# A float32 decoder trunk on one core: four of eight K pairs in seven products, a second block sum by an accumulating transfer, a longer lag at the turns, and grouped half-array products

## The chip, the cores and the metric

The kernel runs on one core of a Trainium2 chip. The metric is the device time of one execution in microseconds, taken as the median of several runs. A profile is one further execution, recorded by the hardware profiler; its rows give the line of the kernel, the engine and the operation. TensorE (PE) multiplies, VectorE (DVE) and ScalarE (ACT) do the work on elements, GpSimd (POOL) does a little of it and issues the accumulating transfers, SyncE (SP) issues the other transfers.

## The reference, cut to what matters

Two decoder layers over 256 tokens of width 2048, in float32. Layer 0 mixes by a chunked state-space scan, layer 1 by differential attention; each is followed by a SwiGLU feed-forward part, with an RMS norm before and after every part.

```python
for i in range(DEPTH):                       # DEPTH = 2
    h = rmsnorm(x, norm_mix_pre[i])
    m = ssd_mixer(h, ...) if i % 2 == 0 else diff_attention(h, ...)
    x = x + rmsnorm(m, norm_mix_post[i])
    h = rmsnorm(x, norm_ffn_pre[i])
    x = x + rmsnorm(swiglu(h, ffn_w_gate[i], ffn_w_up[i], ffn_w_down[i]), norm_ffn_post[i])

def swiglu(h, w_gate, w_up, w_down):         # 2048 -> 5632 -> 2048
    return (jax.nn.silu(h @ w_gate) * (h @ w_up)) @ w_down
```

In the scan, `y_diag` is for each head (width 64) a 128 x 128 matrix of decays times the head's values, for each of two chunks of 128 tokens. In the attention, each of 16 heads has two score matrices of head width 64; their softmaxes are subtracted with a weight.

## The kernel before

**Precision.** Every float32 weight block is cut into two parts in a format that TensorE multiplies in one pass: `hi`, a copy by ACT (L133), and `lo`, the rest, by a subtraction on DVE (L134). Function `prep` does this for one raw tile of up to four blocks of 128 x 512. A product of activations and weights is three matmuls: hi x hi, hi x lo, lo x hi. After the scan, `hi` and `lo` have four buffers each, all preparations use them in turn, and the first operation of a preparation waits until TensorE has done the last product with the tile that held the buffer. Raw tiles come from `raw_tile`: three buffers of `rawp`, and in the feed-forward stage two of `mpool` as well (then the tile is named `rawm`).

**Plain products.** `mv` computes 256 tokens (two token tiles t = 0, 1) against one chunk of 512 columns. The products of t = 0 run as each half tile of weights is ready; those of t = 1 are put in a queue `pending` and run `lag` steps later. So at the end of a chunk the result of t = 0 is complete first. `out_proj` uses `mv` for its last columns (n = 3 for the last one, L719) with the lag it is given, LAG2 = 2; the feed-forward part's first chunk uses LAG = 4. When the last chunk of a token tile is complete, `norm_chain` normalizes it, adds it to the residual stream `x`, transposes it through TensorE (`ptx`) and writes the next activations `xT`; `stats` (L640) sums the squares of the new `x` for the next norm two steps later.

**Products of pairs.** For gate and up (columns 0 to 9 of 11 chunks) and for a part of the down projection, `pair` computes two token tiles x two column chunks at once, a K pair (two blocks of 128 of the contraction) at a time, eight K pairs for gate and up. A plain K pair needs 8 block products, so 24 matmuls. For the K pairs in SEVEN it uses the scheme that multiplies 2 x 2 blocks in seven products, so 21 matmuls: four sums of weight blocks are formed at run time, and four sums of activation blocks, the "forms" (`make_form`, once per layer; `keep` stores them in DRAM, and they are loaded again through POOL's queue at the beginning of parts 1 and 2, L878). The forms live in four buffers with the tag `xr`, which the forms of the down projection use too. The steps of one K pair in seven products are, in `pair`:

- SP loads the four blocks into `raw` (L244); POOL then issues a transfer that adds a block onto `raw[:, 0]` (L247);
- first preparation: `hi` and `lo` of `raw[:, 1:4]` (the blocks as they are, 1536 wide), L259;
- three sums on DVE in place (L261 to L263);
- second preparation: `hi` and `lo` of all of `raw` (the sums, 2048 wide), L264;
- nine matmuls with the first preparation, then twelve with the second. Four of the products go into sums of their own in PSUM (tiles `cp`), the others straight into the results.

After the last K pair in seven products DVE combines the `cp` tiles (L276 to L280), and after K pair 7 `done` adds them to the results; for gate ACT then applies SiLU, for up DVE multiplies. After each up pair the products are transposed into the activations of the down projection (`act_piece`).

**Order.** Weight chunks go in three parts (PARTS): gate and up of some chunks, then the down projection of those, accumulated in DRAM. The order of instructions on each engine is fixed when the program is built; an engine does its own instructions strictly in that order and waits on semaphores. `later(k, fn)` puts work k steps (`tick`) ahead.

**Scan and attention.** `scan_group` runs, interleaved with the products of the next chunks, `diag(0)` at step 6 and `diag(1)` at step 7: 16 small products each whose output is 64 partitions (L543). In `attention_group`, `softmax(t, hp)` computes the scores of two heads of one token tile by products over 64 partitions (L963), masks them, and takes the softmax; it is called for four combinations of t and hp.

```python
            if kp in seven:
                nc.gpsimd.dma_start(raw[:, 0:1], src[0][:, 1:2], accum_op=ALU.add)
```

Of the kernel before, what the change touches and what calls it, by code (L numbers as in the profile page):

```python
# [10 lines left out]
F32 = mybir.dt.float32  # L11
F32R = mybir.dt.float32r
AF = mybir.ActivationFunctionType
ALU = mybir.AluOpType
# [15 lines left out]
LAG = 4  # L30
LAG2 = 2

SEVEN = (2, 4, 6)


PARTS = [((10, 0, 1), (20, 0, 21, 1, 2, 3), {0: (21,), 2: (21, 2)}),
# [5 lines left out]
def trunk_kernel(ctx, tc, x_rows, x_cols, vec_cols, vec64, post_rows, lam_rows,  # L42
# [19 lines left out]
    def aux(name):  # L62
        return auxp.tile([P, 512], F32, tag="aux", name=name)
# [156 lines left out]
    def pair(blocks, stat, seven, form, done):  # L220

        flush()
        acc = {}
        end = len(blocks) - 1  # L230

        def mm(k, st, hi, lo, last):
            first = k not in acc
            if first:
                acc[k] = (auxp.tile([P, 512], F32, tag="aux", name="cp") if isinstance(k, str) else
                          accp.tile([P, 512], F32, tag="acc", name="acc"))
            for q, (a, b) in enumerate(((st[0], hi), (st[0], lo), (st[1], hi))):
                nc.tensor.matmul(acc[k], a, b, start=first and q == 0, stop=last and q == 2)  # L238

        ss = {}  # L240
        for kp, src in enumerate(blocks):
            raw = raw_tile()
            for c in range(2):
                nc.sync.dma_start(raw[:, 2 * c:2 * c + 2], src[c])  # L244
            if kp in seven:

                nc.gpsimd.dma_start(raw[:, 0:1], src[0][:, 1:2], accum_op=ALU.add)  # L247
# [12 lines left out]

            nc.vector.tensor_tensor(raw[:, 2], raw[:, 2], raw[:, 0], op=ALU.add)  # L261
            nc.vector.tensor_tensor(raw[:, 3], raw[:, 3], raw[:, 2], op=ALU.add)  # L262
            nc.vector.tensor_tensor(raw[:, 1], raw[:, 2], raw[:, 1], op=ALU.subtract)  # L263
            sh, sl = prep(raw)  # L264
            mm("p1", stat(kp, 0, 0), hi[:, 1], lo[:, 1], last)
            mm((0, 0), stat(kp, 1, 0), hi[:, 2], lo[:, 2], False)
            mm((0, 1), form(kp, 3), hi[:, 0], lo[:, 0], False)
            tick()
            mm("p6", form(kp, 2), sh[:, 2], sl[:, 2], last)
            mm("p5", form(kp, 0), sh[:, 1], sl[:, 1], last)  # L270
            mm("p7", form(kp, 1), sh[:, 0], sl[:, 0], last)
            mm((1, 0), stat(kp, 1, 1), sh[:, 3], sl[:, 3], False)
            tick()
            if last:
                s1, u, w, x = (t512(n) for n in ("s1", "su", "sw", "sx"))
                nc.scalar.copy(s1, acc["p1"])  # L276
                nc.vector.tensor_tensor(u, acc["p6"], s1, op=ALU.subtract)
                nc.vector.tensor_tensor(w, acc["p5"], u, op=ALU.add)
# [241 lines left out]
    def scan_group(g, st, mts):  # L520
# [59 lines left out]
            nc.vector.tensor_tensor(yo, pyo.rearrange("p (h d) -> p h d", h=8), exb(1), op=ALU.mult)  # L580

        later(5, lambda: (tokens(0), tokens(1)))
        later(6, lambda: (diag(0), to_state()))
        later(7, lambda: (diag(1), turn(0)))
        later(9, new_state)
        later(10, off)
        later(11, lambda: turn(1))
# [27 lines left out]
    def norm_chain(t, ss4, last_mw, step, final, t512):  # L615

        rn = rstd_of(ss4[:, 3:4], D, f"post{step}_{t}", ss4[:, 0:1])
        for n in range(4):
            mw = last_mw if n == 3 else m[(t, n)]
            xt = xres[(t, n)]  # L620
            if final and n == 0:
                nc.scalar.activation(mw, mw, AF.Copy, scale=rn)
                nc.gpsimd.tensor_tensor(xt, xt, mw, op=ALU.add)
            else:
                nc.vector.scalar_tensor_tensor(xt, mw, rn, xt, op0=ALU.mult, op1=ALU.add)  # L625
            if final:
                nc.sync.dma_start(out[t * P:(t + 1) * P, n * 512:(n + 1) * 512], xt)
                continue
            pt = aux("ptx")
            for j in range(4):  # L630
                nc.tensor.transpose(pt[:, j * P:(j + 1) * P], xt[:, j * P:(j + 1) * P], ident)  # L631
            for j in range(4):
                sl = slice(t * P, (t + 1) * P)
                sc = pre_cols[step + 1][:, 4 * n + j:4 * n + j + 1]
                pj = pt[:, j * P:(j + 1) * P]
                nc.scalar.activation(xT_hi[n][:, j, sl], pj, AF.Copy, scale=sc)  # L636
                nc.vector.scalar_tensor_tensor(xT_lo[n][:, j, sl], pj, sc, xT_hi[n][:, j, sl].bitcast(F32),
                                               op0=ALU.mult, op1=ALU.subtract)
# [12 lines left out]
    def out_proj(w, first, last, acts, kgs, step, final, lag, t512, pw, scale=None, ns=range(4), two={}, forms=None, md=None, mid=None):  # L651

# [46 lines left out]
        for n in ns:  # L699
            def evac(t, ps, n=n):  # L700
# [220 lines left out]
    def attention_group(hg):  # L921
# [30 lines left out]

        prT, es, sms = {}, {}, {}

        def softmax(t, hp):
            nk, ts = t + 1, slice(t * P, (t + 1) * P)
            qT, kT = qk[(0, hp)], qk[(1, hp)]

            sc = [aux(f"sc{c}")[:, :2 * nk * P].rearrange("p (h k) -> p h k", h=2) for c in range(2)]
            for h in range(2):  # L960
                for c in range(2):
                    cp = slice(c * 64, (c + 1) * 64)
                    nc.tensor.matmul(sc[c][:, h], qT[cp, h, ts], kT[cp, h, :nk * P], start=True, stop=True)  # L963
            mx = small.tile([P, 2, 2], F32, tag="mx", name="mx", bufs=4)
            sm = small.tile([P, 2, 2], F32, tag="sm", name="sm", bufs=4)
            e = []
            for c in range(2):
                nc.vector.tensor_tensor(sc[c][:, :, ts], sc[c][:, :, ts],
                                        causal.unsqueeze(1).to_broadcast([P, 2, P]), op=ALU.add)
                nc.vector.tensor_reduce(mx[:, c], sc[c], axis=AX.X, op=ALU.max)  # L970
                nc.vector.tensor_scalar(mx[:, c], mx[:, c], qsc[t], -1.0, op0=ALU.mult, op1=ALU.mult)
                e.append(t512("e", (P, 2, nk * P)))
                for h in range(2):
# [3 lines left out]
            for h in range(2):  # L977
# [4 lines left out]
            es[(t, hp)] = e[0]  # L982

        def turn(t, hp):
            nk, e = t + 1, es[(t, hp)]
# [101 lines left out]
```

## Time and profile before

| | us |
|---|---|
| median of 3 runs (2560.80 to 2561.73) | 2561.22 |
| the profiled execution's own time | 2560.26 |
| its span, first to last instruction | 2558.5 |

The span is the time between the first and the last instruction of the record; the 1.8 us around it are start and end. A row of the lists by line has the engine, the operation, the tile written and the tiles read, the shape, the count, then busy time and mean length, then the idle time of the engine before these instructions and who ended it. A row in order of time has start, length, engine, line and operation; what stands in brackets is the idle time before it and what ended it. Two more rows of the page belong to the stages that the change touches, the software queue (the transfers that POOL issues) and the hardware queue:

```profile
q1 hardware_dynamic: 125296, 502.91, 56.8%
q0 software_dynamic: 16416, 33.04, 6.9%
```

The columns are packets, MB, and the time of the packets as a share of the span on 16 DMA engines.

### The profile page before, as it was taken

To read this page: it belongs to the slowest core of one execution; us is meant where nothing else is said; L and a number is where in the kernel's file an instruction comes from. 1 tells how busy PE (TensorE), PEld (TensorE's weight loads), DVE (VectorE), ACT (ScalarE), POOL (GpSimd) and SP (SyncE) were. 2 spreads that over 40 slices of the span, in tenths; PEclk is the share of its full clock that TensorE was granted. 3 is DMA by queue.
4 is the path that set the end of the run, shared out by engine and by line. 5 is a ranking of instruction groups with operands and counts; after the bars stand their busy time and mean duration, and the time that the engine had idled before them with its cause. 6 is when DMAs were issued, how large, how long until landed. Compare 5 with 4: busy or idle time off the path is not lost. (4 is left out here: it accounts for less than half of the span.)

```text
span 2558.5 us, 31249 instructions
## 1 busy us (share of the span) xinstructions
PE 2527.4 (99%) x11860; PEld 2069.1 (81%) x11860; DVE 1908.9 (75%) x2297; ACT 1363.9 (53%) x1656; POOL 237.1 (9%) x222
## 2 busy tenths in 40 slices
PE   9999999999999999999999999999999999999998
PEld 7877888787878888888887778887788888888886
DVE  6777547776687888977886765656578879878985
ACT  5767556665565454554544654444555455545553
POOL 0121000120110000011002100000100000010003
PEclk9999999999999999999999999999999999999999
DMA  7545555454776776777677544444676866796675
GB/s 275 198 165 181 189 191 195 167 180 165 273 259 209 250 242 202 242 235 238 198 244 231 205 147 166 167 157 142 235 227 212 276 217 214 229 261 216 208 248 166
DMA packets 142518, 538.78 MB, mean 211 GB/s; under 512 B 14304, under 2 KB 31008, under 8 KB 114976
## 3 DMA queue, kind: packets, MB, share of 16 engines
q1 hardware_dynamic: 125296, 502.91, 56.8%
q0 software_dynamic: 16416, 33.04, 6.9%
q8 instruction: 93, 1.52, 0.3%
q10 hardware_dynamic: 656, 0.85, 0.1%
q14 instruction: 57, 0.47, 0.1%
HBM read 516.74 MB, written 17.89 MB: 209 GB/s over the span
## 5 line engine op out<-in xcount | busy, mean ns | idle before, releaser
L134 DVE TENSOR_TENSOR lo<-raw,hi 128x2048 fp32r<-128x2048 f32 (+2 forms) x451 | 855.7, 1906 | 381.9 <-ACT hi L133 377.1
L133 ACT CAST hi<-raw 128x2048 fp32r<-128x2048 f32 (+2 forms) x451 | 698.8, 1557 | 600.4 <-DVE raw L263 190.3
L187 PE MATMUL acc<-hi,xT 128*128 128x512 f32 x1792 | 590.3, 400 | 4.7 <-ACT xT L636 2.1
L238 PE MATMUL acc<-hi,xT 128*128 128x512 f32 x1840 | 589.3, 390 | 0.0
L238 PEld LDWEIGHTS acc<-hi,xT 128*128 128x128 f32 x1840 | 345.3, 188 | 71.5
L187 PEld LDWEIGHTS acc<-hi,xT 128*128 128x128 f32 x1792 | 335.8, 188 | 81.1 <-issue 5.9
L238 PE MATMUL acc<-lo,xT 128*128 128x512 f32 x920 | 358.0, 389 | 0.0
L187 PE MATMUL acc<-lo,xT 128*128 128x512 f32 x896 | 352.0, 393 | 1.8 <-DVE lo L134 1.8
L134 DVE TENSOR_TENSOR lo<-rawm,hi 128x2048 fp32r<-128x2048 f32 (+1 forms) x115 | 248.2, 2158 | 71.3 <-ACT hi L133 67.7
L133 ACT CAST hi<-rawm 128x2048 fp32r<-128x2048 f32 (+1 forms) x115 | 207.7, 1806 | 171.3 <-DVE rawm L263 108.4
L238 PEld LDWEIGHTS acc<-lo,xT 128*128 128x128 f32 x920 | 172.7, 188 | 35.6
L187 PEld LDWEIGHTS acc<-lo,xT 128*128 128x128 f32 x896 | 168.8, 188 | 38.4 <-issue 3.6
L238 PE MATMUL acc<-hi,ah_f 128*128 128x512 f32 x468 | 183.1, 391 | 0.0
L238 PE MATMUL acc<-hi,al_f 128*128 128x512 f32 x468 | 182.2, 389 | 0.0
L238 PE MATMUL acc<-lo,ah_f 128*128 128x512 f32 x468 | 182.1, 389 | 0.0
L212 PE MATMUL acc<-xT,hi 128*128 128x512 f32 x512 | 180.1, 397 | 0.0
L238 PE MATMUL cp<-hi,ff 128*128 128x512 f32 x468 | 156.9, 389 | 0.0
L214 PE MATMUL acc<-xT,lo 128*128 128x256 f32 x512 | 142.7, 280 | 0.0
L138 DVE SCALAR_TENSOR_TENSOR lo<-raw,cols,hi 128x512 fp32r<-128x512 f32 x128 | 91.6, 763 | 55.8 <-ACT hi L137 55.7
L212 PEld LDWEIGHTS acc<-xT,hi 128*128 128x128 f32 x512 | 96.1, 188 | 22.9
L137 ACT ACTIVATE hi<-raw,cols 128x512 fp32r<-128x512 f32 x128 | 84.6, 715 | 53.6 <-PE acc L187 36.7
L238 PEld LDWEIGHTS acc<-hi,al_f 128*128 128x128 f32 x468 | 87.8, 188 | 18.2
(279 smaller groups left out, 3491.0 us busy)
## 6 DMA issues: line engine op xcount, KB each, us to landing
raw<-in_w_zxbc_dram SPq DMA_DIRECT2D x80, 1024.0 KB, 4.8
raw<-in_w_d_dram SPq DMA_DIRECT2D x98, 512.0 KB, 5.7
raw<-in_w_g_dram SPq DMA_DIRECT2D x96, 512.0 KB, 5.8
raw<-in_w_u_dram SPq DMA_DIRECT2D x96, 512.0 KB, 5.8
raw<-in_w_qkv_dram SPq DMA_DIRECT2D x48, 1024.0 KB, 4.8
raw<-in_w_so_dram SPq DMA_DIRECT2D x32, 1024.0 KB, 4.8
rawm<-in_w_g_dram SPq DMA_DIRECT2D x64, 512.0 KB, 5.8
rawm<-in_w_u_dram SPq DMA_DIRECT2D x64, 512.0 KB, 6.2
```

The lines of the kernel that those rows point to most:

```text
L133: nc.scalar.copy(hi, raw)
L134: nc.vector.tensor_tensor(lo, raw, hi.bitcast(F32), op=ALU.subtract)
L137: nc.scalar.activation(hi[:, j], raw[:, j], AF.Copy, scale=scale[j])
L138: nc.vector.scalar_tensor_tensor(lo[:, j], raw[:, j], scale[j], hi[:, j].bitcast(F32), op0=ALU.mult, op1=ALU.subtract)
L187: nc.tensor.matmul(acc[t], a, b[:, j], start=(i == 0 and j == 0 and q == 0), stop=(i == last and j == 1 and q == 2))
L212: nc.tensor.matmul(acc[ct], hi[:, j, cs], x.rearrange("p a s -> p (a s)"), start=(i == 0 and j == 0), stop=False)
L214: nc.tensor.matmul(acc[ct][:, :S], lo[:, j, cs], x[:, 0], start=False, stop=(i == last and j == 1))
L238: nc.tensor.matmul(acc[k], a, b, start=first and q == 0, stop=last and q == 2)
```

## The change

SEVEN becomes (1, 3, 4, 6), so each gate pair and each up pair computes four K pairs in seven products and one more form is made and kept per layer. In every K pair in seven products, those of the down projection too, a second accumulating transfer adds `src[0][:, 0]` onto `raw[:, 2]` after the first preparation has read it, and two sums on DVE remain; the places of two of the sums in the tile are exchanged, and so are their uses.

```diff
-SEVEN = (2, 4, 6)
+SEVEN = (1, 3, 4, 6)
...
             hi, lo = prep(raw[:, 1:4])
 
-            nc.vector.tensor_tensor(raw[:, 2], raw[:, 2], raw[:, 0], op=ALU.add)
-            nc.vector.tensor_tensor(raw[:, 3], raw[:, 3], raw[:, 2], op=ALU.add)
-            nc.vector.tensor_tensor(raw[:, 1], raw[:, 2], raw[:, 1], op=ALU.subtract)
+            nc.gpsimd.dma_start(raw[:, 2:3], src[0][:, 0:1], accum_op=ALU.add)
+            nc.vector.tensor_tensor(raw[:, 1], raw[:, 1], raw[:, 2], op=ALU.add)
+            nc.vector.tensor_tensor(raw[:, 3], raw[:, 3], raw[:, 1], op=ALU.add)
             sh, sl = prep(raw)
...
-            mm("p6", form(kp, 2), sh[:, 2], sl[:, 2], last)
-            mm("p5", form(kp, 0), sh[:, 1], sl[:, 1], last)
+            mm("p6", form(kp, 2), sh[:, 1], sl[:, 1], last)
+            mm("p5", form(kp, 0), sh[:, 2], sl[:, 2], last)
```

In the scan, `diag(1)` moves one step earlier, to stand with `diag(0)`. At the turns, the statistics come five steps later instead of two, and the last chunk of the last output projection has the lag 4.

```diff
-        later(6, lambda: (diag(0), to_state()))
-        later(7, lambda: (diag(1), turn(0)))
+        later(6, lambda: (diag(0), diag(1), to_state()))
+        later(7, lambda: turn(0))
...
-            later(2, stats)
+            later(5, stats)
...
-            mv([w[n, kg // 2] for kg in up[::2]], up_stat, evac, lag,
+            mv([w[n, kg // 2] for kg in up[::2]], up_stat, evac, LAG if last and n == 3 else lag,
```

In the attention, `softmax` takes a list of head pairs; for token tile 0 the two calls become one over four heads, with tiles twice as wide, for token tile 1 they stay two.

```diff
-        def softmax(t, hp):
-            nk, ts = t + 1, slice(t * P, (t + 1) * P)
-            qT, kT = qk[(0, hp)], qk[(1, hp)]
+        def softmax(t, hps):
+            nk, ts, nh = t + 1, slice(t * P, (t + 1) * P), 2 * len(hps)
...
-            for h in range(2):
+            for h in range(nh):
+                qT, kT = qk[(0, hps[h // 2])], qk[(1, hps[h // 2])]
...
-        softmax(0, 0)
-        later(1, lambda: softmax(0, 1))
-        later(2, lambda: (turn(0, 0), softmax(1, 0)))
-        later(3, lambda: (turn(0, 1), softmax(1, 1)))
+        softmax(0, (0, 1))
+        later(2, lambda: (turn(0, 0), softmax(1, (0,))))
+        later(3, lambda: (turn(0, 1), softmax(1, (1,))))
```

More of the change, by code (lines that the diff above doesn't have):

```diff
@@ L953, in attention_group @@
         prT, es, sms = {}, {}, {}
-        def softmax(t, hp):
-            nk, ts = t + 1, slice(t * P, (t + 1) * P)
-            qT, kT = qk[(0, hp)], qk[(1, hp)]
-            sc = [aux(f"sc{c}")[:, :2 * nk * P].rearrange("p (h k) -> p h k", h=2) for c in range(2)]
-            for h in range(2):
+        def softmax(t, hps):
+            nk, ts, nh = t + 1, slice(t * P, (t + 1) * P), 2 * len(hps)
+            sc = [aux(f"sc{c}")[:, :nh * nk * P].rearrange("p (h k) -> p h k", h=nh) for c in range(2)]
+            for h in range(nh):
+                qT, kT = qk[(0, hps[h // 2])], qk[(1, hps[h // 2])]
                 for c in range(2):
                     cp = slice(c * 64, (c + 1) * 64)
-                    nc.tensor.matmul(sc[c][:, h], qT[cp, h, ts], kT[cp, h, :nk * P], start=True, stop=True)
-            mx = small.tile([P, 2, 2], F32, tag="mx", name="mx", bufs=4)
-            sm = small.tile([P, 2, 2], F32, tag="sm", name="sm", bufs=4)
+                    nc.tensor.matmul(sc[c][:, h], qT[cp, h % 2, ts], kT[cp, h % 2, :nk * P], start=True, stop=True)
+            mx = small.tile([P, 2, 4], F32, tag="mx", name="mx", bufs=4)[:, :, :nh]
+            sm = small.tile([P, 2, 4], F32, tag="sm", name="sm", bufs=4)[:, :, :nh]
             e = []
@@ L968, in softmax @@
                 nc.vector.tensor_tensor(sc[c][:, :, ts], sc[c][:, :, ts],
-                                        causal.unsqueeze(1).to_broadcast([P, 2, P]), op=ALU.add)
+                                        causal.unsqueeze(1).to_broadcast([P, nh, P]), op=ALU.add)
                 nc.vector.tensor_reduce(mx[:, c], sc[c], axis=AX.X, op=ALU.max)
                 nc.vector.tensor_scalar(mx[:, c], mx[:, c], qsc[t], -1.0, op0=ALU.mult, op1=ALU.mult)
-                e.append(t512("e", (P, 2, nk * P)))
-                for h in range(2):
+                e.append(t512("e", (P, nh, nk * P)))
+                for h in range(nh):
                     nc.scalar.activation(e[c][:, h], sc[c][:, h], AF.Exp, scale=qsc[t], bias=mx[:, c, h:h + 1],
@@ L976, in softmax @@
             nc.vector.reciprocal(sm, sm)
-            for h in range(2):
+            for h in range(nh):
                 nc.vector.tensor_scalar(e[1][:, h], e[1][:, h], sm[:, 1, h:h + 1], neglam,
@@ L981, in softmax @@
                                                op0=ALU.mult, op1=ALU.add)
-            es[(t, hp)] = e[0]
+            for i, hp in enumerate(hps):
+                es[(t, hp)] = e[0][:, 2 * i:2 * i + 2]
         def turn(t, hp):
```

## The prediction

> **What bounds the kernel now.** I read the page first (busy shares, granted clock), then the busy time by stage, then the waits of TensorE, then one pair of weight chunks in order of time on ACT, DVE and PE.
>
> ```profile
> span 2558.5 us, 31249 instructions
> PE 2527.4 (99%) x11860; PEld 2069.1 (81%) x11860; DVE 1908.9 (75%) x2297; ACT 1363.9 (53%) x1656; POOL 237.1 (9%) x222
> PEclk9999999999999999999999999999999999999999
> ```
>
> ```profile
> core 0: us, PE busy (x) PEld busy (x) DVE busy (x) ACT busy (x) POOL busy (x), PEclk, DMA share, GB/s
> 757.20:1372.50 615.30, 614.99 (x2753) 508.97 (x2752) 513.73 (x485) 308.13 (x217) 44.21 (x54) 1.00 0.72 228
> 897.50:939.00 41.50, 41.50 (x185) 34.35 (x183) 33.75 (x28) 19.84 (x13) 2.62 (x3) 1.00 0.79 246
> 980.50:1024.00 43.50, 43.50 (x201) 35.91 (x199) 38.35 (x45) 20.43 (x18) 2.60 (x3) 1.00 0.63 203
> ```
>
> TensorE is busy all the time at full clock. The first window is the whole FFN pair stage of layer 0 (615 us; layer 1 has an equal one). One gate pair or up pair takes 41.5 us (second window); where activations are also turned for the down projection it takes 43.5 and DVE is busy for 38.35 of them (third window). So the end is set by the number of products, as long as ACT and DVE hand over `hi` and `lo` in time. How close that is, one gate pair shows; its columns are start, length, engine and line:
>
> ```profile
> 916.56 0.39 PE L238 MATMUL cp<-hi,xT 128*128 128x512 f32 x1
> ...
> 928.80 0.39 PE L238 MATMUL cp<-hi,ff 128*128 128x512 f32 x1
> 929.02 0.39 PE L238 MATMUL cp<-lo,ff 128*128 128x512 f32 x1
> ```
>
> ```profile
> 916.80 1.48 ACT L133 CAST hi<-rawm 128x1536 fp32r<-128x1536 f32 x1 [2.25 <-issue]
> 922.29 1.92 ACT L133 CAST hi<-rawm 128x2048 fp32r<-128x2048 f32 x1 [4.01 <-DVE rawm L263]
> 924.11 1.90 ACT L133 CAST hi<-raw 128x2048 fp32r<-128x2048 f32 x1
> ```
>
> ```profile
> 918.32 1.76 DVE L134 TENSOR_TENSOR lo<-rawm,hi 128x1536 fp32r<-128x1536 f32 x1 [1.04 <-ACT hi L133]
> 920.11 0.69 DVE L261 TENSOR_TENSOR rawm<-rawm 128x512 f32<-128x512 f32 x1
> 920.84 0.69 DVE L262 TENSOR_TENSOR rawm<-rawm 128x512 f32<-128x512 f32 x1
> 921.45 0.68 DVE L263 TENSOR_TENSOR rawm<-rawm 128x512 f32<-128x512 f32 x1
> 924.24 2.29 DVE L134 TENSOR_TENSOR lo<-rawm,hi 128x2048 fp32r<-128x2048 f32 x1 [2.11 <-ACT hi L133]
> ```
>
> This is K pair 4, in seven products. Successive products start 0.227 us apart (928.80, 929.02), though each is drawn 0.39 long. The first preparation (`hi`, 1536 wide) starts at 916.80, just after PE began the products of another K pair at 916.56 and so was done with a buffer: `hi` and `lo` have four buffers, and a preparation starts when PE releases the fourth before it. From there the chain is `hi` 1.48, `lo` 1.76, three sums 2.0, `hi` of all four 1.92, `lo` 2.29: it ends at 926.53, 9.7 us after its start. PE wants this `lo` at 929.02. **The slack is 2.5 us.** Behind it PE waited almost never:
>
> ```profile
> PE ptx L631 <- DVE x L625: 3.2, 5, 1.5
> PE acc L187 <- ACT xT L636: 2.1, 3, 1.5
> ...
> PE acc L187 <- DVE xT L637: 1.5, 2, 1.1
> ...
> PE cp L238 <- DVE lo L134: 0.3, 1, 0.3
> ```
>
> ```profile
> 1022.27 2.29 DVE L134 TENSOR_TENSOR lo<-rawm,hi 128x2048 fp32r<-128x2048 f32 x1 [2.39 <-ACT hi L133]
> ...
> 1024.62 0.50 PE L238 MATMUL cp<-lo,ff 128*128 128x512 f32 x1 [0.29 <-DVE lo L134]
> ```
>
> The last row is the same place in the window of 43.5 us: there the slack is already nil.
>
> **The change, part by part.** *Products.* A seven-product K pair needs 21 products where a plain one needs 24. SEVEN grows from three to four, in 5 column pairs x gate and up x 2 layers = 20 calls: 60 products less, x 0.227 = **-13.6 us**.
>
> *Work of DVE and ACT.* By the starts in the rows above a seven-product K pair costs DVE 1.79 + 2.0 + 2.21 = 6.0 us now and 1.79 + 1.4 + 2.21 = 5.4 with two sums, a plain one 2.21. A call goes from 5 x 2.21 + 3 x 6.0 = 29.1 to 4 x 2.21 + 4 x 5.4 = 30.4: the transfer does not make DVE lighter than before, it only pays for most of the fourth. ACT gets one more `hi` of 1.48 per call. Both fit in TensorE's time (33.75 + 1.3 of 40.8; 38.35 + 1.3 of 42.8) if nobody waits. The extra form per layer (four small DVE operations and a split, some 3 us) and its reload lie beside products as well; that all four `xr` buffers now hold forms makes the down projection's form wait until the up pair has passed K pair 1, tens of us ahead of its use. I cost these at nothing; uncovered, they would be 2 x 3 us.
>
> *The new wait.* The second accumulating transfer overwrites a block that both halves of the first preparation read, so it is issued after that `lo`, and the two remaining sums wait for its landing. It lies in the chain. Before, the one accumulating transfer came ahead of the first preparation and hid there. Its length stands in the issues by line (count, KB, median us from issue to landing), and the hand-over from DVE to POOL in a wait of another transfer (909.99 + 0.68 to 910.96):
>
> ```profile
> raw<-in_w_g_dram POOLq DMA_DIRECT2D x18, 256.0 KB, 6.2
> raw<-in_w_u_dram POOLq DMA_DIRECT2D x18, 256.0 KB, 4.1
> ...
> raw<-in_w_d_dram POOLq DMA_DIRECT2D x14, 256.0 KB, 7.2
> rawm<-in_w_g_dram POOLq DMA_DIRECT2D x12, 256.0 KB, 5.6
> ...
> rawm<-in_w_u_dram POOLq DMA_DIRECT2D x12, 256.0 KB, 4.2
> ```
>
> ```profile
> 909.99 0.68 DVE L263 TENSOR_TENSOR rawm<-rawm 128x512 f32<-128x512 f32 x1
> ```
>
> ```profile
> 910.96 0.88 POOL L247 DMA_DIRECT2D raw<-in_w_g_dram  x1 [6.60 <-DVE rawm L263]
> ```
>
> The mean over the 60 gate and up transfers is 5.0 us; with 0.3 of hand-over the wait is 5.3, bounded by 4.4 (up) and 6.5 (gate). One sum of 0.6 falls away, so the chain grows by 4.7 to 14.4 us. Against a slack of 2.4 that is an **excess of 2.3 us** for each tight K pair (1.4 to 3.5).
>
> Which are tight: count PE's products from the release of the buffer to the second preparation's first use. With (1, 3, 4, 6) the K pairs 3, 4 and 6 have 21 + 24 + 9 = 54 products, 12.3 us, as K pairs 4 and 6 have today; K pair 1 has 12 + 24 + 24 + 9 = 69, 15.7 us, and just gets through. When PE has waited at 3, K pair 4, whose buffer was free before that, gains as much cover and passes; 6, whose buffer is freed by 3, waits again. Two waits a call: 20 x 2 x 2.3 = **+92 us**. In the crowded calls the slack is nil, but there DVE has other work to put into the wait; I price them like the others (at 4.3 each they would add 32).
>
> The down projection's calls use the same code. Their seven-product K pairs that stand two places after another one have the 54 products too, four a layer; the transfers of `w_d` take 7.2 us: 7.2 + 0.3 - 0.6 - 2.4 = 4.5 us each, x 8 = **+36 us** (0 to 48).
>
> Queues: behind the waiting sums DVE holds the `lo` of later K pairs, PSUM sums and SwiGLU products; behind the waiting transfer POOL holds the first accumulating transfers of later K pairs and the form reloads, needed only for the second `hi`. SP's next loads wait some 5 us longer for a raw buffer, of which there are five. The software queue carries 33.04 MB; 118 transfers of 256 KB more double it, on DMA engines now busy for 0.72 of the stage, so landings get later rather than earlier.
>
> *Lag and statistics at the turns.* The three waits for `x` and `xT` above sum to 6.8 us over the three turns. More products of token tile 1 left over while tile 0 is normalized can cover part: I take **-3** (0 to -7; up to +2 if the longer lag holds `hi` and `lo` back).
>
> *Half-array grouping.* Entering the 64-column products costs 0.32 us (129.38 to 129.70) where the next product otherwise starts after 0.23:
>
> ```profile
> 129.15 0.39 PE L187 MATMUL acc<-lo,xT 128*128 128x512 f32 x1
> 129.38 0.40 PE L187 MATMUL acc<-hi,xT 128*128 128x512 f32 x1
> 129.70 1.09 PE L543 MATMUL py<-mt,xdt 128*64 128x128 f32 x16
> ```
>
> Eight entries fewer in the scan and four in attention: **-1 us** (-3 to +5, if the grouped scores wait for the last K columns in each of four groups). The Trainium skill, TensorEngine Tiling (Array Packing), Key Properties, says that changing the tiling mode drains TensorE; the 0.09 us extra here is what such a drain would come to, so its grouping advice is worth no more than this term.
>
> **Sum**: 92 + 36 - 13.6 - 3 - 1 = +110 us on the profiled execution's own 2560.3 us (its span of 2558.5 and 1.8 around it; the median shown is 1 us more): **2671 us**.
>
> **Rivals.** *The wait is covered* (faster): PE and DVE are given other work meanwhile, such as the nine first products of K pair 4 (2.0 us) ahead of K pair 3's last twelve, or half a plain K pair (2.7 us). That decides when the cover reaches 2.3 us, or the wait falls below 3.0. For it: products into different sums do not depend on each other, and DVE already does another K pair's `lo` between two sums of a call:
>
> ```profile
> 941.36 0.68 DVE L277 TENSOR_TENSOR su<-cp,s 128x512 f32<-128x512 f32 x1
> 941.96 2.28 DVE L134 TENSOR_TENSOR lo<-rawm,hi 128x2048 fp32r<-128x2048 f32 x1
> 944.16 0.69 DVE L278 TENSOR_TENSOR sw<-cp,su 128x512 f32<-128x512 f32 x1
> ```
>
> Against: landings of 4.1 to 7.2 us, and DVE's small reserve. It gives 2560 - 13.6 - 4 = 2543 (2536 to 2555). The Trainium skill, DMA: Bandwidth & Descriptors, Anatomy of one DMA — SWDGE (gpsimd) path, would side with it: 2.0 us plus the bytes at 436 GB/s, an estimate of 2.6 us for 256 KB, below the point above, and thus no excess. This trace disagrees with 4.1 us or more for each of these groups.
>
> *The preparations stay in line* (much slower): if ACT does no later `hi` while it waits for the sums, each seven-product K pair holds it for 1.4 + 1.8 + 5.3 + 1.4 + 1.8 + 0.3 = 12 us.
>
> ```profile
> 1020.33 1.91 ACT L133 CAST hi<-rawm 128x2048 fp32r<-128x2048 f32 x1 [5.51 <-DVE rawm L263]
> ```
>
> That row speaks for it: ACT stood 5.5 us before the second `hi` and took no later one meanwhile; at 922.29 it stood 4.0 us, and the next plain K pair came only at 924.11. A call is then 4 x 1.8 + 4 x 12 = 55 us against 41.5: +13.7 x 20 = +274, with the down projection's 36 and without the 13.6 (TensorE no longer bounds), some 2870 (2790 to 2950). Against it: ACT may have had no better choice there, since the waits were short.
>
> *Hidden just enough* (no change): one wait of 0.7 us a call eats the saving: 2556 to 2566.
>
> **How the numbers follow.** About 0.2% (5 us) is what a measurement of this kernel can tell from no change. Forecast (2600 to 2790, from the bounds of the excess, one to three waits a call) 0.50; covered 0.25; no change 0.06; in line 0.19. So faster 0.25, same 0.06, slower 0.69. The range of 8 in 10 leaves out the line case: 2537 to 2795.
>
> **What would show it.** Right: TensorE waits on `cp` for `lo` (0.3 us now) grow to tens of us, twice a call, and the second sum transfer lands 4 us or more after its issue. Calls of 41 us or less with PE still at 99% would show the cover; calls of 55 us with ACT idle behind the sums would show the line. If landings shrink or the engines' order changes, the excess of 2.3 us is wrong.

## The result, and the profile after

| | us | ratio to before |
|---|---|---|
| before, runs beside these (2560.80 to 2563.17) | 2561.47 | |
| changed (3246.14 to 3250.94) | 3249.04 | 1.2677 [1.2662, 1.2693] |

The kernel is 27% slower, 688 us. The page of the changed kernel (span, busy times, granted clock in 40 slices), its longest waits of TensorE (us in total, times, longest), and the busy times in the window that was the whole feed-forward pair stage of layer 0 before:

```profile
span 3245.8 us, 31519 instructions
PE 2746.9 (85%) x11800; PEld 2178.7 (67%) x11800; DVE 1926.5 (59%) x2269; ACT 1387.7 (43%) x1678; POOL 336.3 (10%) x344
PEclk9999999999898888887889999999898888888888
```

```profile
PE cp L238 <- ACT hi L133: 421.5, 93, 7.4
PE cp L238 <- DVE lo L134: 21.8, 14, 1.8
PE pt_f L291 <- DVE g L824: 13.0, 2, 6.9
```

```profile
core 0: us, PE busy (x) PEld busy (x) DVE busy (x) ACT busy (x) POOL busy (x), PEclk, DMA share, GB/s
757.00:1372.00 615.00, 466.54 (x1750) 361.14 (x1750) 334.57 (x305) 206.19 (x146) 59.82 (x71) 0.86 0.57 165
```

Before, PE was busy for all of that window at full clock; now it is busy for 467 of 615 us at a clock of 0.86, and the stage takes 961 us instead of 615 (first pair product at 759.1, the next plain chunk at 1720.1); in layer 1 it takes 962 instead of 615. So the whole loss lies in the two pair stages, and outside them things got a little better. TensorE waits mostly for `hi` (93 waits, 421.5 us), not for `lo` (14 waits, 21.8 us), and it waits on `cp` 107 times, about once in each of the 98 K pairs in seven products, where the prediction counted two a call and eight in the down projection, 48. The shares of the three engines all fall, PE's from 99 to 85%, DVE's from 75 to 59, ACT's from 53 to 43. When all are less busy at once, look for work that passes from one to the other in a line.

Where the line stands still is seen among the waits of DVE:

```profile
DVE raw L262 <- DMA raw<-in_w_g_dram: 146.1, 24, 8.7
DVE raw L262 <- DMA raw<-in_w_u_dram: 145.1, 24, 9.3
DVE rawm L262 <- DMA rawm<-in_w_g_dram: 108.8, 16, 8.9
DVE rawm L262 <- DMA rawm<-in_w_u_dram: 95.6, 16, 9.5
DVE raw L262 <- DMA raw<-in_w_d_dram: 94.9, 14, 10.9
...
DVE rawm L262 <- DMA rawm<-in_w_d_dram: 34.1, 4, 10.7
```

L262 is the first sum behind the second transfer. It stood still 98 times, once in every seven-product K pair, 624.6 us in all, nine tenths of the loss. One of these in order of time, DVE and then ACT (start, length, engine, line, and the idle time before it):

```profile
1084.72 2.29 DVE L134 TENSOR_TENSOR lo<-raw,hi 128x2048 fp32r<-128x2048 f32 x1 [2.08 <-ACT hi L133]
1086.93 1.75 DVE L134 TENSOR_TENSOR lo<-rawm,hi 128x1536 fp32r<-128x1536 f32 x1
1094.24 0.69 DVE L262 TENSOR_TENSOR rawm<-rawm 128x512 f32<-128x512 f32 x1 [5.56 <-DMA rawm<-in_w_u_dram]
1094.97 0.69 DVE L263 TENSOR_TENSOR rawm<-rawm 128x512 f32<-128x512 f32 x1
1097.75 2.29 DVE L134 TENSOR_TENSOR lo<-rawm,hi 128x2048 fp32r<-128x2048 f32 x1 [2.08 <-ACT hi L133]
```

```profile
1084.60 1.47 ACT L133 CAST hi<-rawm 128x1536 fp32r<-128x1536 f32 x1
1095.82 1.90 ACT L133 CAST hi<-rawm 128x2048 fp32r<-128x2048 f32 x1 [9.76 <-DVE rawm L263]
1097.62 1.89 ACT L133 CAST hi<-raw 128x2048 fp32r<-128x2048 f32 x1
```

DVE ends the first `lo` at 1088.68 and does nothing until the transfer has landed; ACT does nothing from 1086.07 to 1095.82 and takes the next K pair's `hi` (1097.62) only afterwards. Both engines work in program order, and the waiting instruction holds all later preparations. **The length of this line** can be added up by starts. From the first sum to the second `lo` it is 1097.75 - 1094.24 = 3.5 us, then 2.2 to the next `lo`, 1.75 for a first `lo`, and the wait from there to the sum, 6.9 on the mean of the 80 in gate and up: 14.3 us for a seven-product K pair. A plain one puts 2.2 us into the line. The end of a call puts in 8 sums and SwiGLU products (gate) or 12 (up) of 0.6 to 0.7 us, 6.4 on the mean. With the three sums of before, the same sum goes by the rows from 918.32 to 926.45: 8.1 us. Now set this against TensorE's products at 0.227 us, for one call:

| one call of gate or up | line, us | products, us | measured |
|---|---|---|---|
| before: 3 x 8.1 + 5 x 2.2 + 6.4 | 41.7 | 41.5 | 41.9 |
| changed: 4 x 14.3 + 4 x 2.2 + 6.4 | 72.4 | 40.9 | 72.8 |

Measured is the mean of the same four calls of layer 0 (the spacing of their L276 copies). The line gives the new length without TensorE. The row of changed takes its wait of 6.9 us from the same run, so it says where the time lies and does not foretell it; the tests are the runs below. And the line says something of before that the share of busy time did not show: there it was already as long as the products. In these four calls of before DVE was busy for 141.6 us and waited 24.4 for `hi`, 166.0 of 167.5 us:

```profile
897.50:1065.00 167.50, 167.21 (x745) 138.07 (x744) 141.59 (x137) 85.39 (x62) 10.12 (x12) 1.00 0.71 226
```

```profile
DVE lo L134 <- ACT hi L133: 24.4, 15, 2.4
```

### The profile page after: what moved, and what is told of

Read it like the earlier page. It is cut to its first block, busy times and chain, and to the rows that moved or that the text cites. A ratio compares the mean times of both kernels' runs of the same rounds, so it can differ in the third digit from the quotient of the medians.

```text
span 3245.8 us, 31519 instructions
## 1 busy us (share of the span) xinstructions
PE 2746.9 (85%) x11800; PEld 2178.7 (67%) x11800; DVE 1926.5 (59%) x2269; ACT 1387.7 (43%) x1678; POOL 336.3 (10%) x344
## 5 line engine op out<-in xcount | busy, mean ns | idle before, releaser
L133 ACT CAST hi<-raw 128x2048 fp32r<-128x2048 f32 (+2 forms) x463 | 713.2, 1550 | 920.8 <-DVE raw L263 403.6
L134 DVE TENSOR_TENSOR lo<-raw,hi 128x2048 fp32r<-128x2048 f32 (+2 forms) x463 | 870.5, 1889 | 384.0 <-ACT hi L133 378.4
L238 PE MATMUL cp<-hi,ff 128*128 128x512 f32 x588 | 299.5, 573 | 421.5 <-ACT hi L133 421.5
L238 PEld LDWEIGHTS cp<-hi,ff 128*128 128x128 f32 x588 | 155.9, 281 | 491.1 <-ACT hi L133 461.2
L238 PEld LDWEIGHTS acc<-hi,xT 128*128 128x128 f32 x1600 | 328.3, 207 | 112.6 <-ACT hi L133 39.7
L187 PEld LDWEIGHTS acc<-hi,xT 128*128 128x128 f32 x1792 | 335.9, 188 | 74.8 <-issue 4.9
L187 PE MATMUL acc<-lo,xT 128*128 128x512 f32 x896 | 352.7, 394 | 5.4 <-DVE lo L134 5.4
L238 PE MATMUL acc<-lo,xT 128*128 128x512 f32 x800 | 319.5, 399 | 0.0
L262 DVE TENSOR_TENSOR raw<-raw 128x512 f32<-128x512 f32 x62 | 42.9, 692 | 386.0 <-DMA raw<-in_w_g_dram 146.1
L187 PEld LDWEIGHTS acc<-lo,xT 128*128 128x128 f32 x896 | 168.8, 188 | 44.4 <-DVE lo L134 9.7
L238 PE MATMUL cp<-lo,ff 128*128 128x512 f32 x294 | 163.7, 557 | 21.8 <-DVE lo L134 21.8
L238 PEld LDWEIGHTS acc<-lo,xT 128*128 128x128 f32 x800 | 157.3, 197 | 35.3 <-DVE lo L134 0.2
L262 DVE TENSOR_TENSOR rawm<-rawm 128x512 f32<-128x512 f32 x36 | 24.9, 692 | 238.5 <-DMA rawm<-in_w_g_dram 108.8
```

What stands on the lines that cost most here:

```text
L133: nc.scalar.copy(hi, raw)
L134: nc.vector.tensor_tensor(lo, raw, hi.bitcast(F32), op=ALU.subtract)
L187: nc.tensor.matmul(acc[t], a, b[:, j], start=(i == 0 and j == 0 and q == 0), stop=(i == last and j == 1 and q == 2))
L262: nc.vector.tensor_tensor(raw[:, 1], raw[:, 1], raw[:, 2], op=ALU.add)
```

## The experiments

**Four seven-product K pairs alone.** Everything else as before, three sums on DVE.

```diff
-SEVEN = (2, 4, 6)
+SEVEN = (1, 3, 4, 6)
```

> The kernel before with SEVEN = (1, 3, 4, 6) alone: three sums on DVE, no second transfer. Theory in-line (ACT does the preparations strictly in the program's order, so a wait in one holds all later ones): 4 x 1.8 + 4 x 7.2 = 36 us of ACT a call plus some 5 us of sums at its end, about TensorE's 40.9, and two neighbours in seven products (3, 4) that follow each other without a plain K pair between: 2560 to 2680 us. Theory excess (the forecast's: only what the chain exceeds its slack by is lost): the chain stays 9.7 us against a cover of 12.3, so 2548 us. Theory load (the software transfers themselves slow everything): only 20 transfers more, 2548 to 2570 us.

2666.01 us, ratio 1.0398 [1.0368, 1.0428]: +102 us. So the part that was to save 13.6 us loses by itself, with no new transfer. Its waits of TensorE:

```profile
PE cp L238 <- ACT hi L133: 45.4, 24, 3.7
PE acc L238 <- ACT hi L133: 18.8, 43, 1.0
```

The line gives 4 x 8.1 + 4 x 2.2 + 6.4 = 47.6 us a call; the four calls took 47.7. This sum was made up only after the run; ahead of it the line had been put at 36 + 5 us a call, and only the wide range of 2560 to 2680 held. The excess and the load, at 2548 and up to 2570, do not fit: the chain is still the 9.7 us of before under a cover of at least 12.3, and yet the time grows.

**The second transfer alone**, with three seven-product K pairs a call.

```diff
-nc.vector.tensor_tensor(raw[:, 2], raw[:, 2], raw[:, 0], op=ALU.add)
-nc.vector.tensor_tensor(raw[:, 3], raw[:, 3], raw[:, 2], op=ALU.add)
-nc.vector.tensor_tensor(raw[:, 1], raw[:, 2], raw[:, 1], op=ALU.subtract)
+nc.gpsimd.dma_start(raw[:, 2:3], src[0][:, 0:1], accum_op=ALU.add)
+nc.vector.tensor_tensor(raw[:, 1], raw[:, 1], raw[:, 2], op=ALU.add)
+nc.vector.tensor_tensor(raw[:, 3], raw[:, 3], raw[:, 1], op=ALU.add)
```

> The kernel before with the second accumulating transfer alone, SEVEN still (2, 4, 6). In-line: 5 x 1.8 + 3 x 12 = 45 us of ACT a call plus 5 for the sums at its end, 50 against 41.5, so +170 us and more with the down projection and with a lower granted clock: 2750 to 2950 us. Excess: two waits of 2.3 us a call and the down projection's, 2690 us. Load: 156 software transfers for sums instead of 196 in the changed kernel, two thirds of the added transfers, so two thirds of its 688 us: about 3000 us.

3007.57 us, ratio 1.173 [1.1696, 1.1764]: +443 us. This is above the 2750 to 2950 expected of the line and at the load's 3000; what tells these two apart is the next run. With the 6.9 us of the changed kernel in it, the sum gives 3 x 14.3 + 5 x 2.2 + 6.4 = 60.3 a call; the four calls took 57.7, so it is 2.6 too long there.

**The load without the wait.** Four seven-product K pairs with three sums, and the first accumulating transfer issued twice (so that block is added twice): the changed kernel's traffic, but nothing new in the line.

```diff
-nc.gpsimd.dma_start(raw[:, 0:1], src[0][:, 1:2], accum_op=ALU.add)
+for _ in range(2):
+    nc.gpsimd.dma_start(raw[:, 0:1], src[0][:, 1:2], accum_op=ALU.add)
```

> SEVEN = (1, 3, 4, 6) with three sums on DVE, and the first accumulating transfer issued twice, both ahead of the first preparation: as many software transfers as in the changed kernel, none of them in the chain. (The block src[0][:, 1] is added twice, so one of the four sums is not the reference's.) In-line and excess: as the run with four K pairs in seven products alone, within 40 us. Load: near the changed kernel, over 3000 us.

2717.32 us, ratio 1.0598 [1.0567, 1.0629]: 51 us more than four K pairs alone, a little over the 40 allowed for the line and far from the load's 3000. As many transfers cost 51 us when they are issued early, and 583 when the sums stand behind them (3249 less the 2666 of four K pairs alone). Contention is a small part.

**The preparations drawn apart.** The changed kernel, but in gate and up the two preparations of a K pair have others between them (in ORDER, given in short, a is the first, b the second). Products, sums and transfers are the same.

```diff
-SEVEN = (1, 3, 4, 6)
+SEVEN = (1, 2, 4, 5)
+ORDER = 0, 1a, 2a, 3, 1b, 2b, 4a, 5a, 6, 4b, 5b, 7
```

> The changed kernel with the two preparations of a K pair in seven products drawn apart in the program: K pairs 1, 2, 4, 5 in seven products, order 0, 1a, 2a, 3, 1b, 2b, 4a, 5a, 6, 4b, 5b, 7 (a: first preparation, its products and the second transfer; b: sums, second preparation, its products), so at least one other preparation of a plain K pair stands in the wait. Same products, same transfers. In-line: the wait is mostly covered, 2560 to 2720 us. Load: over 3000 us, since the transfers are the same. Excess: 2560 to 2640 us.

2809.91 us, ratio 1.0959 [1.0927, 1.0991]. With as many K pairs in seven products, the order takes back 439 of the 688 us, so it is the line and not the amount of work; but the time stays above the 2560 to 2720 that I had expected. DVE still waits for the second transfer, in gate and up 210.5 us where it was 495.6, and in the down projection, which was not drawn apart:

```profile
DVE raw L271 <- DMA raw<-in_w_d_dram: 99.0, 14, 11.5
DVE raw L271 <- DMA raw<-in_w_u_dram: 78.0, 16, 8.4
...
DVE raw L271 <- DMA raw<-in_w_g_dram: 54.5, 19, 6.6
DVE rawm L271 <- DMA rawm<-in_w_g_dram: 39.5, 12, 7.9
DVE rawm L271 <- DMA rawm<-in_w_u_dram: 38.5, 9, 6.7
```

The rows show why the wait is left. Between the end of a K pair's first `lo` (946.93 in this call) and its sum DVE has one more first `lo` and one plain `lo` to do, 3.9 us; the transfer, issued at 947.78, lands at 955.58, and DVE stands for the rest:

```profile
948.52 2.29 DVE L135 TENSOR_TENSOR lo<-raw,hi 128x2048 fp32r<-128x2048 f32 x1
955.67 0.69 DVE L271 TENSOR_TENSOR raw<-raw 128x512 f32<-128x512 f32 x1 [4.87 <-DMA raw<-in_w_g_dram]
```

**Zero products in the waits.** In the changed kernel the products after a long wait are slow. Three rows behind a wait of 6.3 us, in order of time, and the busy times of three stretches of 4 us around them:

```profile
1047.92 0.63 PE L238 MATMUL cp<-hi,ff 128*128 128x512 f32 x1
1048.35 0.63 PE L238 MATMUL cp<-lo,ff 128*128 128x512 f32 x1
1048.78 0.63 PE L238 MATMUL cp<-hi,ff 128*128 128x512 f32 x1
```

```profile
1044.00:1048.00 4.00, 3.17 (x7) 2.06 (x8) 3.40 (x2) 4.00 (x4) 0.00 (x0) 0.50 0.04 10
1048.00:1052.00 4.00, 4.00 (x15) 3.23 (x14) 4.00 (x4) 2.04 (x2) 0.51 (x1) 0.76 0.94 301
1052.00:1056.00 4.00, 4.00 (x19) 3.30 (x19) 3.77 (x7) 1.47 (x3) 1.24 (x2) 1.00 0.96 300
```

They start 0.43 us apart instead of 0.227, with a granted clock of 0.50, until some 5 us after this wait. The trace has 691 spacings of 0.40 to 0.44 us between products of the pairs (3 before). Is that a loss of its own? In this run TensorE multiplies by zeros while it waits:

```diff
+if len(blocks) == 8:
+    for _ in range(FILL):            # 12
+        nc.tensor.matmul(acc[(0, 0)], stat(kp, 0, 0)[0], zero.to_broadcast([P, 512]), start=False, stop=False)
 mm("p6", form(kp, 2), sh[:, 1], sl[:, 1], last)
```

> The changed kernel with twelve products of a zero (added to an open sum, so it stays the same) between the first nine and the last twelve products of each seven-product K pair of gate and up: 80 places, 12 x 0.227 = 2.7 us each, put where TensorE waits 5 us on the mean. After a wait of over 3 us the products start 0.43 us apart instead of 0.227, for some 4 us. Theory that the granted clock is a loss of its own: with only 2 to 3 us idle left the clock stays full, the slow products (some 690, 140 us, and part of the others) go, and the time falls from 3249 to 3050 to 3150, granted clock 0.97 or more. Rival, the clock only follows the waits and the slow products lie beside ACT's and DVE's line: 3230 to 3280. Rival, the fill itself costs where the wait is short: above 3290.

Three of the five calls of the down projection in a layer have eight K pairs too. The edit therefore also reached twelve of their K pairs in seven products, so it is 92 places and 1104 products, 251 us of them:

```profile
L274 PE MATMUL acc<-zero,xT 128*128 128x512 f32 x960 | 222.7, 381 | 0.0
...
L274 PE MATMUL acc<-zero,ah_f 128*128 128x512 f32 x144 | 33.4, 381 | 0.0
```

```profile
PE cp L241 <- ACT hi L136: 152.8, 65, 6.2
PE cp L241 <- DVE lo L137: 63.5, 47, 1.8
```

3243.32 us, ratio 1.2654 [1.2637, 1.2671]: not told apart from the changed kernel. TensorE's waits for these halves fell from 443 to 216 us, the mean clock rose from 0.914 to 0.947, the slow spacings fell to 476, and the end stayed. A quarter of a millisecond of work was put into TensorE for nothing, so TensorE did not bound the changed kernel, at either clock.

**Three sums in part of the down projection.**

```diff
+if len(blocks) == 8:
     nc.gpsimd.dma_start(raw[:, 2:3], src[0][:, 0:1], accum_op=ALU.add)
     ...
+else:
+    the three sums of before
```

> The changed kernel with the old three sums on DVE in the 18 seven-product K pairs of the down projection; gate and up unchanged. It measures the term that the prediction put at +36 us. Excess over the slack in four K pairs a layer: 3249 - 36 = 3213 (3200 to 3249). Line of preparations there as well: each of the 18 stands the 7 us from lo to sum, less the 0.6 of the sum saved, and some clock after it: 3249 - 18 x 7 = 3120 (3090 to 3160).

For the same reason only the six seven-product K pairs of the calls with six got three sums. 3208.63 us, ratio 1.2518 [1.2501, 1.2535]: 41 us less, by chance what had been expected of four tight K pairs a layer. It says 6.8 us for each of the six.

**Three sums in all of it.** The condition now names the calls of gate and up.

```diff
+gate_up = len(blocks) == 8 and len(seven) == len(SEVEN)
```

> The changed kernel with three sums on DVE in all 18 seven-product K pairs of the down projection (the run before this one of that name reached only the six in calls of six K pairs, and gave 40 us). Line: each gives about the 6.8 us that those six gave, 3249 - 122 = 3127 (3100 to 3155). Excess as predicted, with four tight K pairs a layer: 3213, which the six alone have passed; the other twelve give nothing then: 3200 to 3215.

3151.62 us, ratio 1.2293 [1.2276, 1.231]: 98 us less than the changed kernel, 5.5 for each of 18 on the mean. The six of the run before cost 6.8 each and the other twelve 4.7, so the loss is not that of eight tight K pairs alone.

**The first sum on DVE.** It halves the transfers that the software queue carries for the K pairs.

```diff
-nc.gpsimd.dma_start(raw[:, 0:1], src[0][:, 1:2], accum_op=ALU.add)
 ...
+nc.vector.tensor_tensor(raw[:, 0], raw[:, 0], raw[:, 1], op=ALU.add)
 nc.vector.tensor_tensor(raw[:, 1], raw[:, 1], raw[:, 2], op=ALU.add)
```

> The changed kernel with its first accumulating transfer, the one issued ahead of the first preparation, replaced by a sum on DVE behind the first lo: 98 transfers less on the software queue, 98 sums of 0.7 us on DVE more, in time in which DVE waits for the second transfer. In the changed kernel the sum starts 5.6 us after the end of lo where the second transfer is alone (45 in gate and up) and 8.5 us where it was issued right behind another K pair's first one (35). Theory that the queue makes it longer: the 35 fall to 5.6, 3249 - 35 x 2.9 = 3150 (3100 to 3180). Rival, the transfer takes that long by itself: 3220 to 3270. Theory of the line alone says nothing on this and holds either way.

3175.46 us, ratio 1.2391 [1.2375, 1.2408]: 73 us less, in spite of 98 sums more. From the end of `lo` to the sum behind the transfer it now takes 6.1 us on the mean of gate and up (80), where it was 5.6 for the 45 transfers that were alone and 8.5 for the 35 right behind another. DVE's waits for the transfer, two rows of this kernel:

```profile
DVE raw L260 <- DMA raw<-in_w_u_dram: 113.9, 24, 9.6
DVE raw L260 <- DMA raw<-in_w_g_dram: 111.4, 24, 6.5
```

With the down projection's they fall from 624.6 to 475.1. That is 150 us; the added sums take 0.6 each in the same line, some 60, and of the 90 left 73 show. The time lies in the range that the queue was given, but the 35 places fell only from 8.5 to 7.0 us and not to 5.6; the other 45 fell to 5.4. So standing behind another transfer makes up about half of what these 35 had been longer by; why they still take longer than the others is not shown.

**One seven-product K pair a call.** Meant as a test between a slack that each K pair has for itself and one line for all: the kernel before with a single seven-product K pair a call, which does its sums by the second transfer.

```diff
-SEVEN = (2, 4, 6)
+SEVEN = (4,)
```

> The kernel before with one seven-product K pair a call (4) instead of three, its sums by the second transfer; the down projection in three sums. Products alone: 2 x 3 x 0.227 x 20 = +27 us, 2589. Theory of one full line: the line of a call is 13.0 (one K pair with a lone second transfer: 1.8 + 2.2 + 1.75 + 5.6 + 1.6) + 7 x 2.2 + 6.5 = 35 us against 42.9 of products; it has room and the wait costs nothing: 2589 (2580 to 2600). The prediction's excess, in which each tight K pair has its own slack of 2.5 us: the chain grows by 5.6 - 0.6 = 5.0, so 2.5 us of each of 20 waits show: 2589 + 50 = 2640 (2620 to 2660).

2588.42 us, ratio 1.0096 [1.0082, 1.011], the 2589 of the line and not the 2640 that this run put down to the excess. Among its waits of TensorE none for a seven-product sum (`cp`) is left; the longest is elsewhere:

```profile
PE acc L187 <- DVE lo L134: 5.5, 4, 1.8
```

An uncrowded call takes 42.8 us, its products 42.9, so a wait of 5 us from `lo` to sum costs nothing here. But the run does not tell the two accounts apart. Counted as the prediction counts, K pair 4 alone has 3 x 24 + 9 = 81 products between the release of its buffer and the second preparation's first use, 18.4 us, where the tight K pairs have 54; a chain of 14.4 us goes into that, so the prediction's own excess is nil as well. One of the 20 places in order of time, the release and the use:

```profile
1002.55 1.48 ACT L133 CAST hi<-raw 128x1536 fp32r<-128x1536 f32 x1 [2.10 <-PE acc L238]
```

```profile
1021.82 0.39 PE L238 MATMUL cp<-lo,ff 128*128 128x512 f32 x1
```

In all 20 the second `lo` is ready 1.1 to 5.3 us ahead of its product. What does tell them apart is the run with four K pairs alone, where the chain was within its slack and time was lost all the same.

**The small parts alone**: lag and statistics at the turns, and the half-array grouping, on the kernel before.

> The kernel before with only the lag and the later statistics at the turns and the half-array grouping; the pairs as before. It measures the terms of -3 and -1 us. As predicted: 2561.5 - 4 = 2557.5 (2551 to 2562). Rival, the products left over hold hi and lo back, or the grouped scores wait: 2562 to 2570. No theory of the pairs says anything on it.

2557.52 us, ratio 0.9976 [0.9967, 0.9986]: -6 us, together.

**Three sums, drawn apart.** Two kernels that the line points to: four seven-product K pairs, three sums on DVE, the small parts, and preparations that are not in line. The first has one K pair between a and b at most places:

```diff
+SEVEN = (1, 3, 5, 6)
+ORDER = 0, 1a, 2, 1b, 3a, 4, 3b, 5a, 6a, 5b, 6b, 7
```

> Four seven-product K pairs (1, 3, 5, 6) with three sums on DVE and no second transfer; the two preparations of a K pair have another K pair's preparation between them in gate and up (order 0, 1a, 2, 1b, 3a, 4, 3b, 5a, 6a, 5b, 6b, 7); turns and grouping as changed. Theory of one full line: in DVE's order a call is, by rows of the changed kernel, 4 x (lo 1.75 + sums 2.0 + lo 2.2) + 4 x 2.2 + 6.5 for the end of the call = 39.1 us when no ACT cast stands in it, against 40.8 of products: TensorE bounds again, 2561.5 - 13.6 - 6 = 2542 (2535 to 2555). Theory that a fourth seven-product K pair is too much work for DVE wherever it is put: like the four sevens in line, 2600 to 2670. Between: the crowded calls wait, 2555 to 2600.

2554.58 us, ratio 0.9962 [0.9949, 0.9976], at the upper end of the line's range and some 10 us short of the gain that it gave; TensorE still waits 9.5 us on `cp`. So the fourth K pair is not too much work for DVE. The second has the order of the run with preparations apart:

> The kernel drawn apart in the order 0, 1a, 2a, 3, 1b, 2b, 4a, 5a, 6, 4b, 5b, 7 as in the run with preparations apart, but with three sums on DVE in place of the second transfer (in the down projection too). Against that run's 2810 it shows what the second transfer costs when it is out of the line. Line alone: the order takes it out of the way, so both were equal but for the down projection's 120: 2690. Second transfer still costs by its queue and by the raw buffers that it holds: 2540 to 2600 here.

**2544.48 us, ratio 0.9929 [0.9916, 0.9941]**: the fastest kernel here, 18 us below before. Its page, and its busy times in the window of the pair stage:

```profile
span 2542.3 us, 31321 instructions
...
PE 2508.8 (99%) x11800; PEld 2058.9 (81%) x11800; DVE 1969.8 (77%) x2367; ACT 1399.9 (55%) x1678; POOL 253.6 (10%) x246
```

```profile
757.00:1372.00 615.00, 614.37 (x2749) 508.25 (x2748) 549.81 (x528) 328.59 (x229) 54.76 (x66) 1.00 0.76 240
```

An uncrowded call takes 40.8 us, the length of its products. DVE is busy for 550 of 615 us, more than in any kernel above, and TensorE doesn't wait for it: with the order changed, ACT's casts lie beside DVE's work instead of between its steps. What ACT waits for here is TensorE's release of a buffer:

```profile
935.15 1.91 ACT L134 CAST hi<-raw 128x2048 fp32r<-128x2048 f32 x1 [3.23 <-PE acc L239]
937.87 1.49 ACT L134 CAST hi<-rawm 128x1536 fp32r<-128x1536 f32 x1 [0.81 <-PE acc L239]
940.59 1.49 ACT L134 CAST hi<-raw 128x1536 fp32r<-128x1536 f32 x1 [1.24 <-PE acc L239]
```

Against the same order with the second transfer (2810) it is 265 us, where the line had been expected to leave only the down projection's 120, since the wait was taken as covered. It was not: in that run DVE waited for second transfers for 210.5 us in gate and up and for 137.0 in the down projection, which was not drawn apart. Drawing apart by 3.9 us does not cover the transfer; how much of its length is its place in POOL's queue, and what the raw buffers cost that it holds longer, was not taken apart.

## Why the prediction was wrong

The direction was right, the size was not: +110 us forecast, 688 measured, outside the range. Part of the direction was luck: four K pairs alone, which the prediction booked as a gain of 13.6 us, lose 102.

*The step that failed* is "Against a slack of 2.4 that is an excess of 2.3 us for each tight K pair", and with it "Two waits a call". It gives every K pair a slack of its own, as if each wait began anew with 2.4 us in hand, and lets a plain K pair or an earlier wait refill it. But all preparations pass through one line of ACT and DVE, and that line was full: 41.7 us a call against 41.5 of products. What is added to a full line shows in the time whole, in every K pair, tight or not: with four K pairs alone no chain was longer than before and a call took 5.8 us more (47.7 against 41.9), and in the down projection both the six K pairs of the shorter calls and the other twelve cost (6.8 and 4.7 us each), where eight had been counted. The run with one seven-product K pair a call is no evidence for this step, since both accounts give no loss there.

*"Both fit in TensorE's time (33.75 + 1.3 of 40.8 ...) if nobody waits"* was the same mistake in the work of DVE and ACT. It compared busy time. Of the 41.5 us of a call DVE was busy for 33.75, but most of the rest were its waits for `hi` inside a K pair (2.11 us in the row at 924.24), and these belong to the line. So the fourth K pair, costed at nothing, cost 102 us by itself.

*Price of the wait.* Forecast 5.3 us, within 4.4 to 6.5; measured from the end of `lo` to the sum 5.6 where the transfer was alone, 8.5 behind another, 6.9 on the mean of gate and up. This is not what failed: with 6.9 in its sum the prediction's two waits a call would have come to 40 x (6.9 - 0.6 - 2.4) = 156 us instead of 92. The sentence that landings "get later rather than earlier" was right and should have gone into the price.

*Down projection.* Forecast +36; all 18 K pairs together cost 98.

*Crowded calls.* The 4.3 us in the prediction's bracket do not follow from its rows: with no slack the whole growth of 4.7 would show, and the bracket would be 38 us instead of 32. This changes nothing in the account.

*Products.* Forecast -13.6. TensorE did 60 matmuls less, but it bounded nothing any more. Where it does bound, the term holds: from the small parts alone to the fastest kernel the ratio falls from 0.9976 to 0.9929, 12 us.

*Turns and grouping.* Forecast -4 together, measured -6 (-8.5 to -3.6); the two were not measured apart. The "grouping advice" that the prediction speaks of is its own conclusion from the drain.

*The rivals.* "The preparations stay in line" was the right mechanism, with a chance of 0.19 and a call of 55 us against 72.8 measured. What its sum left out is in the table above: the first `lo` waits for the second `lo` of the K pair before (a seven-product K pair is 14.3 us, not 12, with the longer wait), and the end of a call stands in the same line. Its own test, ACT idle behind the sums, is what the trace shows. The argument against it, that ACT "may have had no better choice", was none: the starts of one call of before would have shown that `hi` and `lo` are taken in program order everywhere, and that the line's sum is as long as the call. "The wait is covered" fell; nothing was moved into the wait. The 2.6 us that the Trainium skill's fit gave for the transfer (DMA: Bandwidth & Descriptors, Anatomy of one DMA — SWDGE (gpsimd) path) were not seen either: lone ones took 5.3 us from issue to the sum.

## What to carry to other kernels

Where two engines hand work to and fro in program order, add up their line over a whole loop, with the waits inside it, and compare that with the bounding engine's time; a share of 81% busy can be a full line. A slack seen at one place is not one for each place. Before a step is put on a slower path to relieve an engine, look at what stands behind it in program order, and draw its two ends apart by more than the path takes: here 3.9 us of other work did not cover the transfer, and the fourth K pair gained only with the sums left on DVE and the preparations drawn apart. And count a test by the account that it is to refute before it is run: the run with one K pair could not refute the excess.

## What the runs showed of the hardware

After each of the changed kernel's 81 waits of TensorE of 3 us and more the granted clock was 0.50, until 3.0 to 8.5 us after the end of the wait, and 512-column products started 0.427 us apart. The Trainium skill, TensorE: Matmul & The Clock Gate, says in its section Wait — 56ns, not 53.3ns? that these products start 426.7 ns apart while the array is cold; the trace agrees. Three us is no threshold: some stretches at 0.50 had only waits of 1.8 to 2.9 us ahead of them. The slow products cost nothing here: with a third of the slow spacings gone the time was the same, since another line set it.

The sum behind an accumulating transfer of 256 KB started 5.3 us after the transfer's issue when that was alone (45 of them), and 7.1 us when it was issued right behind another (35); with the other one taken away, these same 35 still took 6.7 and the rest 5.1. Issued early, the added transfers cost no more than 51 us in all.
